# End of a decoder block: the last residual half rows added into the PSUM banks, outputs by one fused operation, third pass tile by tile

## The chip, the cores and the metric

The kernel runs on one core of a Trainium2 chip. The metric is device microseconds of one execution. The kernel before took a median of 804.33 us over three runs (804.27 to 804.5). The core has five engines that work beside each other: TensorE (PE in the profile; PEld are its weight loads) multiplies into PSUM banks, VectorE (DVE) and ScalarE (ACT) do element work and can read and write PSUM, GpSimd (POOL) helps early in the kernel, and SyncE (SP) issues nearly all DMAs.

## The reference, cut to what matters

One decoder block on 512 tokens of width 1024: token mixers, then a SwiGLU feed-forward layer, then a final norm. The change concerns the last product and the final norm alone:

```python
def rmsnorm(x, g):
    y = x * rsqrt(mean(x * x, axis=-1, keepdims=True) + EPS)
    return y * g
...
x = x + m @ w_mix_out                                   # residual stream, 512 x 1024
h = rmsnorm(x, norm2_g)
x = x + (silu(h @ ffn_w1) * (h @ ffn_w3)) @ ffn_w2      # ffn_w2 is 2816 x 1024
return rmsnorm(x, norm_f_g)
```

All of it is float32.

## The kernel before, in words

**Products.** Each float32 operand is split into a high part (rounded to a format that TensorE multiplies fast) and a low part (the rest): `split_to` makes the high part by a copy on ACT (L122) and the low part by a subtraction (L118), for the weights of the end on DVE. A product of two tiles is then three matmuls: high times high, high times low, low times high.

**The last product** (`Sevenfold` with `outq`) is a two by two block product done with seven block products instead of eight. The 512 tokens are four tiles of 128; tiles 0 and 1 are the upper block row and tiles 2 and 3 the lower one. The 1024 output columns are two halves, h = 0 and 1, of 512 columns, the size of one PSUM bank. The inner dimension has 11 steps (k = 0 to 10). The weights are quarters of ffn_w2 (`b11`, `b21`, `b22`, ...) and sums of quarters (`t1` to `t4`) that the kernel made much earlier and stored in DRAM. Weights come through a ring of four raw buffers and a ring of five split buffers, one chunk after the other in a fixed order (`wchunk`, `get`, `weights`).

`run` makes three passes over k. The first fills banks `r1`, `r2` and `r5` (two banks each, i = 0 and 1). The second (`second`) goes on in `r1` with `t2`, and fills a new `r2` and `r7`. The third (`third`) goes on in `r1` with `t4`. What stands in `r1[i]` after each pass is part of a different output: after the third it is the product for token tile 2 + i, column half 0.

`x2[t][h]` (the profile's `x2b`) holds the residual stream of token tile t and column half h, reloaded from DRAM. `plus(t, h, bank)` adds a bank to it on DVE (`add`, L883).

**The end** (`out_end`, L1202 to L1225) runs after the first pass: `second`; then the sums that tiles 0 and 1 still lack; then `finish(0)` and `finish(1)`; then `r7` is added to tiles 2 and 3; then the third pass with k from 0 to 7, each k for tile 2 and then tile 3; and at last, for tile 2 and then tile 3, `finish` with `rest`, which runs the third pass for k = 8, 9, 10 and adds `r1[i]` to column half 0.

**`finish(t)`** (L1178 to L1200) is the final norm of one token tile. `rstd_of` takes the sum of squares of the two halves on ACT (`Square` with `accum_out`, L534 and L540, each followed by a read of the accumulator), forms the mean plus epsilon (DVE L535), takes the root on ACT (L541) and the reciprocal on DVE (L542). Each half is multiplied by the gain `gf` on DVE (L1184) before the reciprocal is known, and by the reciprocal afterwards: one half on DVE (L1194), the other on ACT (L1198), for tile 2 both on DVE (L1196). Two DMAs of 256 KB store the tile (L1200, issued by SP).

**What sets the order.** The order of instructions on each engine is fixed when the program is built; a planner orders them by the order of writing and its own estimates. Each engine then takes its list strictly in order and waits where an operand is not there. SP's list of DMAs is in order too, and the output stores are the last in it.

Of the kernel before, what the change touches and what calls it, by code (L numbers as in the profile page):

```python
# [8 lines left out]
F32 = mybir.dt.float32  # L9
F32R = mybir.dt.float32r  # L10
AF = mybir.ActivationFunctionType
ALU = mybir.AluOpType
# [34 lines left out]
ADDING = ()  # L47
SUMS_FROM, SUMS_AHEAD = 5, 3
GATES_AT = 6
SUMS_AT, SUMS_STEP, SUMS_LAG, STORE_LAG = 4, 3, 2, 4  # L50


# [33 lines left out]
def tile_block(ctx, tc, a, out):  # L86
# [9 lines left out]
    def tiles(tag, bufs):  # L96
        p_ = pool(tag, bufs)
        return lambda name, dtype=F32: p_.tile([P, T], dtype, tag=tag, name=name)

    longt, shortt, gatet = tiles("long", SLOTS), tiles("short", SHORT), tiles("gate", GATES)  # L100

    def pairt(name, dtype=F32R):

        return longt(f"{name}h", dtype), longt(f"{name}l", dtype)

    def bank(name):
        return psum.tile([P, T], F32, tag="mm", name=name)
# [4 lines left out]
    vec, act, pe, pool_e = nc.vector, nc.scalar, nc.tensor, nc.gpsimd  # L112


    newest = {}

    def sub(eng, o, x, y):
        return eng.tensor_tensor(out=o, in0=x, in1=y, op=ALU.subtract)  # L118

    def split_to(h, l, full, eng, copy=act.copy):  # L120

        copy(h, full)  # L122
        last = sub(eng, l, full, h.bitcast(F32))
        if eng is pool_e:
            newest["sub"] = last.ins
        return h, l

    def split(name, full, eng, p_=None, copy=act.copy):
        p_ = p_ or pairt(name)
        return split_to(*p_, full, eng, copy)  # L130
# [9 lines left out]
    def emit_chunk():  # L140
        if emitted[0] == GATES_AT:
            load_gates()
        key, src, kt, cols, where, lo, after = chunks[emitted[0]]
        emitted[0] += 1
        n = kt * cols
        if where == "made":
            raw = src()
        else:
            raw = raws.tile([P, 1024], F32, tag="raw", name=f"raw_{key}")
        rv = raw[:, :n]  # L150
        if where == "made":
            pass
        elif callable(src):
            src(raw)
        else:
            newest["load"] = nc.sync.dma_start(rv.rearrange("p (k n) -> p k n", k=kt), src).ins
        if where != "long":
            hl = hls.tile([P, 2, 1024], F32R, tag="hl", name=f"hl_{key}")
            h, l = split_to(hl[:, 0, :n], hl[:, 1, :n], rv, lo)
            if after:  # L160
                after(rv, h)
            held[key] = (h.rearrange("p (k n) -> p k n", k=kt), l.rearrange("p (k n) -> p k n", k=kt))
        else:
            held[key] = [
                split_to(longt(f"{key}h{i}", F32R), longt(f"{key}l{i}", F32R), rv[:, i * T : (i + 1) * T], lo)
                for i in range(2)
            ]
# [25 lines left out]
    def load_gates():  # L193
      with tc.issue_after(newest["load"]):
        for gi, name in enumerate(("lru_wa", "lru_wx")):
            nc.sync.dma_start(gate_rows[:, gi, :], a[name][0].rearrange("h r n -> (h r) n"))
# [205 lines left out]
    outq = Quartered("o", a["ffn_w2"][0].rearrange("(k p) n -> p k n", p=P), NF // 2, vec)  # L402
# [89 lines left out]
    first = [i for i, (lo, _, _) in enumerate(parts) if lo < n_first]  # L492
# [36 lines left out]
    def rstd_begin(half, junk):  # L529

        i = n_stats[0]
        n_stats[0] += 1
        ss, r = stats[:, i, :2], stats[:, i, 2:3]
        act.activation(junk, half, AF.Square, accum_out=ss[:, 0:1])  # L534
        vec.tensor_scalar(out=ss[:, 0:1], in0=ss[:, 0:1], scalar1=1.0 / D, scalar2=EPS, op0=ALU.mult, op1=ALU.add)  # L535
        return ss, r

    def rstd_end(begun, half, junk):
        ss, r = begun
        act.activation(junk, half, AF.Square, accum_out=ss[:, 1:2])  # L540
        act.activation(r, ss[:, 1:2], AF.Sqrt, scale=1.0 / D, bias=ss[:, 0:1])  # L541
        vec.reciprocal(r, r)  # L542
        return r

    def rstd_of(halves, junk, between=None):
        begun = rstd_begin(halves[0], junk[0])
        if between:
            between()
        return rstd_end(begun, halves[1], junk[1])
# [318 lines left out]
    for j in range(8):  # L868
        ws = w_tiles(f"lo{j}_0", 5) + w_tiles(f"lo{j}_1", 5)
        ps = bank(f"yb{j}")  # L870
# [12 lines left out]
    add = lambda o, x, y: vec.tensor_tensor(out=o, in0=x, in1=y, op=ALU.add)  # L883
# [100 lines left out]
    for n, j in enumerate(mixq.order()):  # L984
        ws = w_tiles(f"co{j}", ND)
        ps = bank(f"ya{j}")
        mm3(ps, ws, un)
        o = sga[j]
# [6 lines left out]
    x2 = [[longt(f"x2{t}{h}") for h in range(2)] for t in range(NT)]  # L995
# [66 lines left out]
    first = {}  # L1062
# [104 lines left out]
    x2 = [[longt(f"x2b{t}{h}") for h in range(2)] for t in range(NT)]  # L1167
    gf = pairt("gf", F32)
# [6 lines left out]
        for h in range(2):  # L1175
            nc.sync.dma_start(gf[h], a["norm_f_g"][h * T : (h + 1) * T].partition_broadcast(P))

    def finish(t, rest=None):  # L1178

        h = 1 if rest else 0  # L1180
        o = [shortt(f"of{t}{i}") for i in range(2)]

        def scaled(i):
            vec.tensor_tensor(out=o[i], in0=x2[t][i], in1=gf[i], op=ALU.mult)  # L1184

        def between():
            scaled(h)
            if rest:
                rest()
            scaled(1 - h)  # L1190

        r = rstd_of([x2[t][h], x2[t][1 - h]], [bank(f"jk{t}{i}") for i in range(2)], between)

        vec.tensor_scalar(out=o[1 - h], in0=o[1 - h], scalar1=r, scalar2=None, op0=ALU.mult)  # L1194
        if t == 2:
            vec.tensor_scalar(out=o[h], in0=o[h], scalar1=r, scalar2=None, op0=ALU.mult)  # L1196
        else:
            act.activation(o[h], o[h], AF.Copy, scale=r)  # L1198
        for i in (1 - h, h):
            nc.sync.dma_start(o_nat[:, t, i * T : (i + 1) * T], o[i])  # L1200

    def out_end(second, plus, r1, r2, r7, third):  # L1202
        kh, hold = outq.kh, 3
        second()
        for i in range(2):
            plus(i, 1, r1[i])
            plus(i, 1, r2[i])
            plus(2 + i, 1, r1[i])
        for i in range(2):
            finish(i)  # L1210
        for i in range(2):
            for h in (1, 0):
                plus(2 + i, h, r7[i])
        for k in range(kh - hold):
            for i in range(2):
                third(i, [k])
        for k in range(kh - hold, kh):
            outq.get(k, "t4")
        for i in range(2):

            def rest():
                third(i, range(kh - hold, kh))
                plus(2 + i, 0, r1[i])

            finish(2 + i, rest)  # L1225

    o7.run(x2, loads, out_end)


# [31 lines left out]
```

## Time and profile before

| what | value |
|---|---|
| median of three runs | 804.33 us (804.27 to 804.5) |
| the profiled execution | 805.56 us |
| its span in the trace | 803.8 us |
| PE busy | 790.0 us, 98% of the span |
| DVE busy | 678.6 us, 84% |
| ACT busy | 471.8 us, 59% |
| mean granted TensorE clock | 0.996 |

Times in the trace are microseconds from the start of the span. The profiled execution took 1.8 us more than its span (what lies around the traced instructions) and 1.2 us more than the median. PE is busy almost throughout, so the kernel's length is PE's work plus what stands before its first and after its last matmul. A row of a timeline reads: start, duration, engine, line, operation, output<-inputs, shape, and in brackets how long the engine sat idle before it and what ended the wait. Consecutive operations of DVE and of ACT overlap a little, so two rows can start closer together than one row is long.

### The profile page before, as it was taken

The page shows a single profiled execution, that of the slowest core. Times are in us where ns is not written, and L with a number is a line of the kernel's source. Part 1 is how long each engine was busy: PE and PEld are TensorE (multiplying, and loading weights), DVE is VectorE, ACT ScalarE, POOL GpSimd, SP SyncE. Part 2 cuts the span into 40 slices and gives each one's busy share as a digit, 9 for nine tenths or more (in the row PEclk, how much of TensorE's full clock was granted, in tenths as well). Part 3 has the DMA queues.
Part 4 walks back from the last instruction along what each step waited for, and adds up shares of the span by engine and source line. Part 5 has one row for each costly group of instructions (what it writes and reads, how often), then busy time and mean ns, then how long its engine had stood idle before and what let it go on. Part 6 is the DMA issues. An engine that isn't in the chain of part 4 may idle for free.

```text
span 803.8 us, 12199 instructions
## 1 busy us (share of the span) xinstructions
PE 790.0 (98%) x4374; PEld 690.7 (86%) x4374; DVE 678.6 (84%) x1034; ACT 471.8 (59%) x677; POOL 232.8 (29%) x182
## 2 busy tenths in 40 slices
PE   8999999999999999999999999999999999999996
PEld 7988888878888888888888888999999999888885
DVE  4699999999989988795887889977878887899756
ACT  7446595888668864573335574555455555577443
POOL 3565857686865855130000000000000000000000
PEclk9999999999999999999999999999999999999999
DMA  7845556477565764358947536467655553676652
GB/s 216 229 124 166 161 162 192 126 219 216 165 196 153 218 181 135 116 188 266 291 150 248 172 106 183 116 163 195 157 132 132 132 132 105 214 258 196 198 169 105
DMA packets 184624, 140.29 MB, mean 175 GB/s; under 512 B 14279, under 2 KB 162163, under 8 KB 184563
## 3 DMA queue, kind: packets, MB, share of 16 engines
q1 hardware_dynamic: 183123, 134.27, 55.7%
q0 software_dynamic: 1440, 5.24, 3.5%
q8 instruction: 34, 0.56, 0.3%
q14 instruction: 27, 0.22, 0.1%
HBM read 113.79 MB, written 18.64 MB: 165 GB/s over the span
## 4 chain that ended last, share of the span: by engine, by line
PE 82%; DVE 8%; DMA 4%; ACT 2%; SPq 1%; issue 1%; POOL 1%; ACTq 0%; POOLq 0%; DVEq 0%
PE z L518 28%; PE or L930 13%; PE ft L1057 7%; PE yb L518 7%; PE fa L1057 6%; PE ya L518 5%; PE mxr L930 5%; PE fe L1057 3%; PE fr L1057 3%; DVE cv L677 2%; PE fb L1057 2%; PE g L804 2%; DMA raw_in<-in_w_in_dram 2%; PE f L518 1%; DMA raw_fb<-in_ffn_w_dram 1%
## 5 line engine op out<-in xcount | busy, mean ns | idle before, releaser
L677 DVE SCALAR_TENSOR_TENSOR cv<-u,par,cv 128x511 f32<-128x511 f32 (+16 forms) x240 | 162.2, 730 | 2.7 <-ACT cv L674 2.5
L118 POOL TENSOR_TENSOR hl_in<-raw_in,hl_in 128x1024 fp32r<-128x1024 f32 x52 | 125.9, 2428 | 82.4 <-ACT hl_in L122 80.7
L344 POOL DMA_DIRECT2D raw_fb<-raw_fb x10 | 8.8, 875 | 300.0 <-DVE raw_fb L346 188.1
L118 POOL TENSOR_TENSOR ows<-ows 128x256 f32<-128x256 f32 x66 | 57.6, 875 | 37.1 <-DMA ows<-in_ffn_w_dram 34.1
L122 ACT CAST hl_in<-raw_in 128x1024 fp32r<-128x1024 f32 x52 | 54.2, 1043 | 11.5 <-PE z L518 6.6
L122 ACT CAST hl_ft<-raw_fb 128x1024 fp32r<-128x1024 f32 x40 | 41.9, 1049 | 31.2 <-DVE raw_fb L346 16.8
L118 DVE TENSOR_TENSOR hl_ft<-raw_fb,hl_ft 128x1024 fp32r<-128x1024 f32 x40 | 48.6, 1220 | 8.8 <-ACT hl_ft L122 8.7
L518 PE MATMUL z<-h10h,hl_in 128*128 128x512 f32 (+1 forms) x112 | 42.5, 381 | 1.5 <-ACT hl_in L122 1.2
L118 DVE TENSOR_TENSOR hl_fb<-raw_fb,hl_fb 128x1024 fp32r<-128x1024 f32 x30 | 36.6, 1221 | 8.7 <-ACT hl_fb L122 8.5
L518 PE MATMUL z<-h11h,hl_in 128*128 128x512 f32 (+1 forms) x112 | 41.9, 376 | 0.0
L518 PE MATMUL z<-h13h,hl_in 128*128 128x512 f32 (+1 forms) x112 | 41.9, 375 | 0.0
L518 PE MATMUL z<-h12h,hl_in 128*128 128x512 f32 (+1 forms) x112 | 41.9, 375 | 0.0
L518 PE MATMUL z<-h15h,hl_in 128*128 128x512 f32 (+1 forms) x112 | 41.8, 374 | 0.0
L518 PE MATMUL z<-h17h,hl_in 128*128 128x512 f32 (+1 forms) x112 | 41.7, 374 | 0.0
L518 PE MATMUL z<-h16h,hl_in 128*128 128x512 f32 (+1 forms) x112 | 41.7, 374 | 0.0
L518 PE MATMUL z<-h14h,hl_in 128*128 128x512 f32 (+1 forms) x112 | 41.7, 374 | 0.0
L346 DVE TENSOR_TENSOR raw_fb<-raw_fb,raw_fb 128x1024 f32<-128x1024 f32 x20 | 24.5, 1225 | 18.9 <-DMA raw_fb<-in_ffn_w_dram 18.7
L122 ACT CAST hl_fb<-raw_fb 128x1024 fp32r<-128x1024 f32 x30 | 31.4, 1046 | 6.9 <-PE mxr L930 3.7
L122 ACT CAST hl_ob<-raw_ob 128x1024 fp32r<-128x1024 f32 (+1 forms) x23 | 23.3, 1015 | 20.2 <-PE or L930 9.7
L118 DVE TENSOR_TENSOR hl_ob<-raw_ob,hl_ob 128x1024 fp32r<-128x1024 f32 (+1 forms) x23 | 27.0, 1174 | 9.5 <-ACT hl_ob L122 6.7
L1057 PE MATMUL fe<-hs_0h,hl_ft 128*128 128x256 f32 x160 | 30.8, 284 | 0.5 <-DVE hl_ft L118 0.5
L1057 PE MATMUL ft<-hs_1h,hl_ft 128*128 128x256 f32 x160 | 30.4, 284 | 0.0
(961 smaller groups left out, 2618.9 us busy)
## 6 DMA issues: line engine op xcount, KB each, us to landing
raw_in<-in_w_in_dram SPq DMA_DIRECT2D x52, 512.0 KB
raw_fb<-in_ffn_w_dram SPq DMA_DIRECT2D x96, 256.0 KB
ows<-in_ffn_w_dram SPq DMA_DIRECT2D x44, 256.0 KB
os<-ows SPq DMA_DIRECT2D x22, 512.0 KB
raw_ob<-in_ffn_w_dram SPq DMA_DIRECT2D x33, 256.0 KB
raw_ot<-os SPq DMA_DIRECT2D x33, 256.0 KB
raw_lo<-in_lru_w_out_dram SPq DMA_DIRECT2D x16, 320.0 KB
raw_fb<-raw_fb POOLq DMA_DIRECT2D x10, 512.0 KB, 4.5
```

The costliest lines, as they stand in the source:

```text
L118: return eng.tensor_tensor(out=o, in0=x, in1=y, op=ALU.subtract)
L122: copy(h, full)
L344: pool_e.dma_start(out=q, in_=y, accum_op=ALU.add)
L346: vec.tensor_tensor(out=q, in0=q, in1=y, op=ALU.add)
L518: pe.matmul(ps, l, r, start=i == 0, stop=i == n - 1)
L677: vec.scalar_tensor_tensor(out=acc[c][:, s:], in0=u[c][:, : T - s], scalar=dw(c, s), in1=acc[c][:, s:], op0=ALU.mult, op1=ALU.add)
L804: pe.matmul(ps, l, r, start=k == 0, stop=k == len(mms) - 1)
L930: pe.matmul(banks[i], l_[:, ts], r_, start=start and n == 0, stop=stop and n == 2, skip_group_check=again)
L1057: pe.matmul(ps[:, HALVES[i]], lw[:, 4 * i + c, :], rx_, start=not (again or i or c or m), stop=bool(i and c == 3 and m == 2), skip_group_c ...
```

## The change

Four things are edited; all of them lie in the end of the kernel.

1. **Third pass in blocks, tile by tile.** k = 0 to 3 for tile 2, then for tile 3; k = 4 to 7 for tile 2, then for tile 3. Before, the two tiles took turns at every k. The last block, k = 8 to 10, was and stays tile by tile.
2. **Residual into the bank.** `r7` is added to all four half rows of tiles 2 and 3 at once, half 0 first. After the block k = 0 to 3 of tile 2 + i, `x2[2 + i][0]` is added into the bank `r1[i]` on DVE; TensorE then goes on adding k = 4 to 10 to it. So at the end the bank holds the finished row half, and the addition after the last matmul is gone. The splits of later weights on DVE are held behind the first of these additions (`newest["tie"]`).
3. **Norm read from the bank, outputs fused.** `finish` for tiles 2 and 3 squares the half row out of the bank, and makes the output by one `scalar_tensor_tensor` (row times reciprocal times gain) instead of a `tensor_tensor` and a `tensor_scalar`. For tiles 2 and 3 the other half is still multiplied by the gain ahead of time and by the reciprocal on ACT; for tiles 0 and 1 both halves are fused operations on DVE.
4. **`finish(0)` and `finish(1)` moved** from before the third pass to after its block k = 4 to 7. The output tiles come from the large pool (`longt`) instead of the small one (`shortt`).

```diff
+SEED_AT = 4
...
     def split_to(h, l, full, eng, copy=act.copy):
         copy(h, full)
-        last = sub(eng, l, full, h.bitcast(F32))
+        if eng is vec and "tie" in newest:
+            with tc.issue_after(newest["tie"]):
+                last = sub(eng, l, full, h.bitcast(F32))
+        else:
+            last = sub(eng, l, full, h.bitcast(F32))
...
-    def finish(t, rest=None):
-        h = 1 if rest else 0
-        o = [shortt(f"of{t}{i}") for i in range(2)]
-        def scaled(i):
-            vec.tensor_tensor(out=o[i], in0=x2[t][i], in1=gf[i], op=ALU.mult)
-        def between():
-            scaled(h)
-            if rest:
-                rest()
-            scaled(1 - h)
-        r = rstd_of([x2[t][h], x2[t][1 - h]], [bank(f"jk{t}{i}") for i in range(2)], between)
-        vec.tensor_scalar(out=o[1 - h], in0=o[1 - h], scalar1=r, scalar2=None, op0=ALU.mult)
-        if t == 2:
-            vec.tensor_scalar(out=o[h], in0=o[h], scalar1=r, scalar2=None, op0=ALU.mult)
+    def finish(t, ps=None, rest=None):
+        o = [longt(f"of{t}{i}") for i in range(2)]
+        jk = [bank(f"jk{t}{i}") for i in range(2)]
+        first = x2[t][0] if ps is None else ps
+        begun = rstd_begin(x2[t][1], jk[0])
+        if rest:
+            vec.tensor_tensor(out=o[1], in0=x2[t][1], in1=gf[1], op=ALU.mult)
+            rest()
+        r = rstd_end(begun, first, jk[1])
+        vec.scalar_tensor_tensor(out=o[0], in0=first, scalar=r, in1=gf[0], op0=ALU.mult, op1=ALU.mult)
+        if rest:
+            act.activation(o[1], o[1], AF.Copy, scale=r)
         else:
-            act.activation(o[h], o[h], AF.Copy, scale=r)
-        for i in (1 - h, h):
+            vec.scalar_tensor_tensor(out=o[1], in0=x2[t][1], scalar=r, in1=gf[1], op0=ALU.mult, op1=ALU.mult)
+        for i in (0, 1):
             nc.sync.dma_start(o_nat[:, t, i * T : (i + 1) * T], o[i])
...
-        for i in range(2):
-            finish(i)
-        for i in range(2):
-            for h in (1, 0):
+        for h in (0, 1):
+            for i in range(2):
                 plus(2 + i, h, r7[i])
-        for k in range(kh - hold):
+        for k in range(SEED_AT):
+            outq.get(k, "t4", ahead=1)
+        for ks in (range(SEED_AT), range(SEED_AT, kh - hold)):
             for i in range(2):
-                third(i, [k])
+                third(i, ks)
+                if ks[0] == 0:
+                    seed = add(r1[i], r1[i], x2[2 + i][0])
+                    if i == 0:
+                        newest["tie"] = seed.ins
+        finish(0)
         for k in range(kh - hold, kh):
             outq.get(k, "t4")
+        finish(1)
         for i in range(2):
-            def rest():
-                third(i, range(kh - hold, kh))
-                plus(2 + i, 0, r1[i])
-            finish(2 + i, rest)
+            finish(2 + i, r1[i], lambda: third(i, range(kh - hold, kh)))
```

## The prediction

> **What bounds the kernel now.** I read the page first (shares of the engines, the chain that ended last), then the chain over the last 64 us in order of time, then the timelines of PE, DVE, ACT and SP from 780 us on, and at last the transfers in short windows behind the last matmul.
>
> ```profile
> PE 82%; DVE 8%; DMA 4%; ACT 2%; SPq 1%; issue 1%; POOL 1%; ACTq 0%; POOLq 0%; DVEq 0%
> ```
>
> ```profile
> 739.65 55.26 PE or L930 x241
> 794.91 0.02 issue
> 794.93 0.70 DVE x2b L883
> ...
> 796.97 0.28 DVE x2b L883
> ...
> 799.28 0.72 ACT of L1198
> ```
>
> The chain runs on PE without a break from 739.65 to 794.91. From there it goes over DVE and ACT to the last output tile. So only two things can move the time here: a new hole in PE before its last matmul, or the length of the tail behind it.
>
> ```profile
> 781.34 0.39 PE L930 MATMUL or<-hl_ot,oeb10l 128*128 128x512 f32 x1
> 781.72 0.70 PE L930 MATMUL or<-hl_ot,ovb0h 128*128 128x512 f32 x2
> ...
> 794.50 0.39 PE L930 MATMUL or<-hl_ot,ovb10l 128*128 128x512 f32 x1
> 794.73 0.62 PE L930 MATMUL or<-hl_ot,ovb8h 128*128 128x512 f32 x2
> ...
> 796.54 0.39 PE L930 MATMUL or<-hl_ot,ovb10l 128*128 128x512 f32 x1
> ```
>
> PE, one row each: the second pass ends, the third starts at 781.72, tile 2 ends with the matmul at 794.50, tile 3 with that at 796.54. From 794.50 to 796.54 are nine matmuls, 0.227 us each; a block of four k (12 matmuls) is 2.72 us, and the whole third pass (66) fills 781.72 to 796.77.
>
> The tail, first on DVE and ACT:
>
> ```profile
> 794.93 0.69 DVE L883 TENSOR_TENSOR x2b<-or,x2b 128x512 f32<-128x512 f32 x1 [2.86 <-PE or L930]
> ...
> 796.97 0.69 DVE L883 TENSOR_TENSOR x2b<-or,x2b 128x512 f32<-128x512 f32 x1
> ...
> 798.70 0.48 DVE L1196 TENSOR_SCALAR of<-of,stats 128x512 f32<-128x512 f32 x1
> 799.10 0.15 DVE L542 RECIPROCAL stats<-stats 128x1 f32<-128x1 f32 x1
> 799.29 0.49 DVE L1194 TENSOR_SCALAR of<-of,stats 128x512 f32<-128x512 f32 x1
> ```
>
> ```profile
> 796.29 0.58 ACT L534 ACTIVATE jk<-x2b 128x512 f32<-128x512 f32 x1
> 796.81 0.19 ACT L534 ACTIVATION_READ_ACCUMULATOR jk<-x2b 128x1 f32 x1
> 796.90 0.28 ACT L541 ACTIVATE stats<-stats 128x1 f32<-128x1 f32 x1
> 797.70 0.60 ACT L540 ACTIVATE jk<-x2b 128x512 f32<-128x512 f32 x1 [0.51 <-DVE x2b L883]
> 798.23 0.19 ACT L540 ACTIVATION_READ_ACCUMULATOR jk<-x2b 128x1 f32 x1
> 798.45 0.29 ACT L541 ACTIVATE stats<-stats 128x1 f32<-128x1 f32 x1
> 799.28 0.72 ACT L1198 ACTIVATE of<-of,stats 128x512 f32<-128x512 f32 x1 [0.54 <-DVE stats L542]
> ```
>
> After PE: add (796.97), square (797.70), root (798.45), reciprocal (799.10, late because DVE still scales tile 2 at 798.70), then both halves of tile 3 are scaled, on DVE until 799.78 and on ACT until 800.00. Then the stores (SP's rows, and windows whose last two columns are the busy share of the DMA engines and GB/s):
>
> ```profile
> 798.81 0.33 SPq L1200 DMA_DIRECT2D out_dram<-of  x1
> 799.24 0.90 SPq L1200 DMA_DIRECT2D out_dram<-of  x2
> 800.22 0.40 SPq L1200 DMA_DIRECT2D out_dram<-of  x1
> ```
>
> ```profile
> 799.00:799.60 0.60, 0.00 (x0) 0.00 (x0) 0.56 (x3) 0.32 (x1) 0.00 (x0) 1.00 0.00 0
> 799.60:800.00 0.40, 0.00 (x0) 0.00 (x0) 0.17 (x1) 0.40 (x1) 0.00 (x0) 1.00 0.91 333
> 800.80:801.20 0.40, 0.00 (x0) 0.00 (x0) 0.00 (x0) 0.00 (x0) 0.00 (x0) 0.78 1.04 379
> 802.00:802.40 0.40, 0.00 (x0) 0.00 (x0) 0.00 (x0) 0.00 (x0) 0.00 (x0) 0.50 0.96 364
> 802.40:802.80 0.40, 0.00 (x0) 0.00 (x0) 0.00 (x0) 0.00 (x0) 0.00 (x0) 0.50 0.07 21
> ```
>
> This is the part that the engines' shares hide: all four stores of tiles 2 and 3 are issued between 798.81 and 800.22, 0.42 us apart at the closest, and the data flow at some 380 GB/s without a gap from about 799.65 to 802.42. That is 2.77 us for four stores, 0.69 each: they queue, so the end goes by the first of the four, not by the last. Data start 0.84 us after an issue (798.81 to 799.65), and the span ends at 803.78, 1.36 after the last data.
>
> **The change, part by part.**
>
> *Third pass in blocks.* The same 66 matmuls in another order: 0 on PE, as long as each block finds its weights and its bank. Blocks on PE: tile 2 k0–3 781.72 to 784.44, tile 3 to 787.16, tile 2 k4–7 to 789.88, tile 3 to 792.60, then k8–10 as before. The split buffer that k = 10 reuses is free once tile 3 has done k = 1, now at about 785.8; its copy on ACT then ends near 786.6 and is wanted at 793.97. SP's list of loads has the same order and the same waits; no load moves.
>
> *Additions and seeds on DVE.* The page of time around them:
>
> ```profile
> 780.29 3.08 DVE L883 TENSOR_TENSOR x2b<-or,x2b 128x512 f32<-128x512 f32 x5
> 783.29 0.68 DVE L1184 TENSOR_TENSOR of<-x2b,gfl 128x512 f32<-128x512 f32 x1
> ...
> 788.46 2.95 DVE L118 TENSOR_TENSOR hl_ot<-raw_ot,hl_ot 128x1024 fp32r<-128x1024 f32 x3
> ```
>
> ```profile
> L883 DVE TENSOR_TENSOR fa<-fa,se 128x512 f32<-128x512 f32 x6 | 4.2, 692 | 0.0
> ```
>
> Five additions take 3.08 us, one every 0.60. The changed list has the four `r7` additions next: 783.29 to 785.69. The first seed follows. The trace has an addition into its own bank (`fa`, 692 ns), so the seed runs 785.69 to 786.38. PE saw a bank 0.15 us after DVE's last read of it (the second of the five additions, 780.89 to 781.57, then PE at 781.72), so PE may go on in that bank from 786.53 and wants it at 787.16: 0.63 us in hand. Behind the seed, in DVE's order, wait the splits of the later weights. k = 6 and 7 (1.2 us by the last row's three splits, two whole and one half): 786.3 to 787.5, its low part wanted at 788.75. The second seed can start when tile 3's block is through PE, near 787.4, and ends by 788.1, wanted at 789.88. The other two splits end near 789.9, wanted at 792.8 and 794.2. All of it is hidden behind PE; price 0, with 0.63 us as the thinnest cover. If that cover goes, each microsecond of delay is one on PE.
>
> *Norms of tiles 0 and 1, moved.* On DVE three small operations, two reciprocals, four fused operations and one gain product:
>
> ```profile
> L741 DVE SCALAR_TENSOR_TENSOR u<-z,par,sg x8: 741/748/750, 39.1 to 235.7; 128x512 f32<-128x512 f32 x8
> ```
>
> A fused operation of this size, out of a bank with a second operand, takes 748 ns, so the five large ones take some 3.5 us from 789.9, to about 793.8 with the small ones; DVE is next wanted at 796.2. The four squares on ACT fit into the time before 794.93, where ACT stood idle for 8.5 us before. Their four stores go out between about 791 and 794 and need 2.8 us of transfers, so they are through before tile 2's. Price 0; the cover is PE's last 3 us, and without it each fused operation would cost about 0.65.
>
> *The add after the last matmul, gone.* The built order on ACT at the end is: square of tile 2's bank, square of tile 3's other half, root of tile 2, scaling of tile 2's half 1, square of tile 3's bank, root, scaling. No row squares out of a bank; a copy of the same size out of a bank is a bound from below and the square from SBUF one from above:
>
> ```profile
> L1148 ACT COPY fb<-fa x6: 570/570/580, 571.1 to 671.3; 128x512 f32<-128x512 f32 x6
> ```
>
> 0.57 against 0.60 us; I take the square's own pace. Tile 2's bank is readable at 794.93 (where DVE started on it). Squares at 794.93 and 795.56 (796.29 less 795.66 is 0.63 a piece), root at 796.19. A root to a reciprocal that finds DVE free shows at the kernel's start:
>
> ```profile
> 5.65 0.29 ACT L541 ACTIVATE stats<-stats 128x1 f32<-128x1 f32 x1
> 5.97 0.16 DVE L542 RECIPROCAL stats<-stats 128x1 f32<-128x1 f32 x1 [1.47 <-ACT stats L541]
> ```
>
> 0.32 us. So reciprocal 796.51, and 0.18 later (799.10 to 799.28) ACT's scaling of tile 2 at 796.69 and DVE's fused operation beside it, both done near 797.43. ACT is free again 0.61 after, at 797.30. Tile 3's bank is readable at 796.97, so here the change adds a wait of 0.33 us: the square of tile 3 stands behind tile 2's scaling on ACT. Then square 797.30, root 798.06 (+0.76, as from 797.70 to 798.45), reciprocal 798.38 with DVE free, scaling on both engines at 798.57: ACT until 799.29, DVE (0.75 in place of 0.49) until 799.32. Before: 800.00. The add's 0.73 and DVE's delay of about 0.33 are saved, 0.33 is given back.
>
> *Stores.* Tile 2's are issued at 797.45 and 797.87 and flow from 798.29 to 799.68. Tile 3's are issued at 799.32 and 799.74, flow from 800.16 and, 2 x 0.69 later, end at 801.55. With 1.36 behind it the span ends at 802.91, 0.87 less than 803.78. The profiled execution, 805.56 with its span of 803.78, would become 804.69; it stands 1.23 above the median of 804.33, to which I apply the same difference: **803.46**.
>
> *A rule on stores.* The row shows stores that queue at 380 GB/s. The Trainium skill ("DMA: Bandwidth & Descriptors", the section on the anatomy of one DMA) gives each DMA, on GpSimd's path, a fixed cost of about 2.0 us, most of it the confirmation of the last byte, plus its bytes at 436 GB/s. By that rule the end would hang on the last issue rather than on the first, which is the second rival below; the trace's gapless 2.77 us speak for the queue.
>
> **Rivals.**
>
> *Seed too late, slower.* If the first seed is released only when tile 3's block is through as well (one wait for the whole group of PE work), it starts at 787.36, ends at 788.05, and PE goes on in the bank at 788.20 in place of 787.16: 1.04 us of hole, against 0.87 of gain, 804.50. In general PE is touched once the seed ends 0.63 late, and the kernel is slower than before from 1.50 late. For it speaks that PE already waits for DVE at this place (781.57 to 781.72) and that the cover is thin; against it, that the seed stands in DVE's list ahead of anything that needs tile 3's block. A further late seed would add to it; 0.05 for this, of which 0.04 over the bound.
>
> *The end follows the last issue.* If what ends the kernel is the last store's own latency, only its issue counts: 800.22 becomes 799.74, a gain of 0.48, **803.85**. The gapless transfer speaks against it. 0.13.
>
> *ACT not in the way.* If tile 3's square runs as soon as its bank is ready (796.97), everything after it is 0.33 earlier: 803.13. The built order speaks against it; some slack in each of the chained waits could give as much. 0.10.
>
> *More than the tail's gain.* From the last matmul's start to the span's end are 7.24 us, and without any wait on ACT the steps still need 6.04. To win over 1.6 us, something ahead of PE's end has to move too, of which there is only the hole of 0.15 at 781.57. 0.05.
>
> **How the numbers follow.** The forecast has the rest, 0.67, and its own range is 803.2 to 803.7. The range over the cases takes in the third and the second rival and half a microsecond of a late seed: 802.9 to 804.2. A measurement of this kernel can tell about 0.2% from no change, 1.6 us; the forecast and the middle rivals lie within that: same 0.91, faster 0.05, slower 0.04.
>
> **What would show it.** Right: no row of PE waiting on DVE between 781.8 and 796.8; last matmul still near 796.5; first seed done near 786.4; ACT's square of tile 3 starting 0.3 after its bank is ready; two separate bursts of transfers, the last ending near 801.55. Wrong: a hole in PE at 787.2 or 789.9, DVE still at tile 1's fused operations after 796.2, or a span that ends other than 1.36 after the last data.

## The result and the profile after

The changed kernel takes a median of 803.38 us (802.25 to 804.39, 21 runs) against 804.33 us (803.24 to 806.04, 21 runs) before: a ratio of 0.9986, with a 95% interval of 0.9980 to 0.9992. That is 0.95 us less; 0.87 was forecast. The interval leaves out 1, so the gain is real, and it lies within the 0.2% that the prediction took as the bound of no change.

The profiled execution took 803.2 us with a span of 801.42 us, 2.36 less than the 803.78 before. Not all of this is the change. The two timelines show where the difference arises. First PE after the change: end of the second pass, start of the third, tile 3's last matmul before PE returns to tile 2's bank and the return itself, last matmul of tile 2 and of tile 3.

```profile
779.91 0.39 PE L935 MATMUL or<-hl_ot,oeb10l 128*128 128x512 f32 x1
780.28 0.70 PE L935 MATMUL or<-hl_ot,ovb0h 128*128 128x512 f32 x2
...
785.59 0.39 PE L935 MATMUL or<-hl_ot,ovb3l 128*128 128x512 f32 x1
785.81 0.62 PE L935 MATMUL or<-hl_ot,ovb4h 128*128 128x512 f32 x2
...
793.07 0.39 PE L935 MATMUL or<-hl_ot,ovb10l 128*128 128x512 f32 x1
...
795.11 0.39 PE L935 MATMUL or<-hl_ot,ovb10l 128*128 128x512 f32 x1
```

The third pass starts 1.44 us earlier than before (780.28 against 781.72), and up to there the two kernels are the same. This part is chance: the profiled execution before took 1.23 us more than its kernel's median, the one after 0.18 less, and 0.96 of the 1.44 us stand there by the 308th of the 4374 matmuls, far ahead of the edits. Among the ten further profiles below, the third pass starts anywhere from 779.47 to 782.96. From its start to the last matmul are 14.83 us (before 14.82), and from the start of the last matmul to the end of the span 6.31 us (before 7.24). So the change is worth 0.93 us in the trace, all of it in the tail. Below, this **tail**, and the **third pass** from its first to its last matmul, are what the experiments are read by: they repeat to some hundredths, while the medians of ten runs move by some tenths for reasons that lie ahead of the change.

DVE after the change, in the third pass and the tail:

```profile
778.86 5.46 DVE L888 TENSOR_TENSOR x2b<-or,x2b 128x512 f32<-128x512 f32 x9
784.24 0.69 DVE L888 TENSOR_TENSOR or<-or,x2b 128x512 f32<-128x512 f32 x1
784.84 1.21 DVE L119 TENSOR_TENSOR hl_ot<-raw_ot,hl_ot 128x1024 fp32r<-128x1024 f32 x1
786.01 0.70 DVE L888 TENSOR_TENSOR or<-or,x2b 128x512 f32<-128x512 f32 x1
786.62 1.82 DVE L119 TENSOR_TENSOR hl_ot<-raw_ot,hl_ot 128x1024 fp32r<-128x1024 f32 x2
...
791.92 0.68 DVE L1190 TENSOR_TENSOR of<-x2b,gfl 128x512 f32<-128x512 f32 x1
...
796.89 0.16 DVE L547 RECIPROCAL stats<-stats 128x1 f32<-128x1 f32 x1 [0.33 <-ACT stats L546]
797.09 0.75 DVE L1193 SCALAR_TENSOR_TENSOR of<-or,stats,gfh 128x512 f32<-128x512 f32 x1
```

The rows `or<-or,x2b` are the two seeds. They take 0.69 and 0.70 us, the rows around them are the additions and splits between which the built order has them, and DVE has done everything for tiles 0 and 1 by 792.0, and tile 2's gain product by 792.6. Nothing is left between the last matmul and ACT's square. ACT in the tail:

```profile
793.49 0.58 ACT L545 ACTIVATE jk<-or 128x512 f32<-128x512 f32 x1 [4.47 <-PE or L935]
...
795.21 0.72 ACT L1195 ACTIVATE of<-of,stats 128x512 f32<-128x512 f32 x1 [0.23 <-DVE stats L547]
795.84 0.58 ACT L545 ACTIVATE jk<-or 128x512 f32<-128x512 f32 x1
796.35 0.18 ACT L545 ACTIVATION_READ_ACCUMULATOR jk<-or 128x1 f32 x1
796.56 0.29 ACT L546 ACTIVATE stats<-stats 128x1 f32<-128x1 f32 x1
797.09 0.72 ACT L1195 ACTIVATE of<-of,stats 128x512 f32<-128x512 f32 x1 [0.23 <-DVE stats L547]
```

Tile 2's bank is squared 0.42 us after its last matmul started (793.07 to 793.49). Tile 3's is squared 0.73 after (795.11 to 795.84): ACT scales tile 2 in between. Then the stores, in windows whose last columns are the busy share of the DMA engines and GB/s:

```profile
797.00:797.40 0.40, 0.00 (x0) 0.00 (x0) 0.36 (x2) 0.31 (x1) 0.00 (x0) 1.00 1.05 394
...
798.20:798.60 0.40, 0.00 (x0) 0.00 (x0) 0.00 (x0) 0.00 (x0) 0.00 (x0) 0.70 0.04 10
798.60:799.00 0.40, 0.00 (x0) 0.00 (x0) 0.00 (x0) 0.00 (x0) 0.00 (x0) 0.50 0.81 297
...
799.80:800.20 0.40, 0.00 (x0) 0.00 (x0) 0.00 (x0) 0.00 (x0) 0.00 (x0) 0.50 0.62 231
800.20:801.40 1.20, 0.00 (x0) 0.00 (x0) 0.00 (x0) 0.00 (x0) 0.00 (x0) 0.50 0.00 0
```

There are two bursts now, tile 2's and tile 3's, with a hole between them at 798.2 to 798.6, where before four stores ran on without one. The last data move at about 800.06, and the span ends 1.36 us later, as before. (Ends of data are read from the windows' shares, as if all DMA engines stopped together; the record of the last single packet ends some 0.1 us later in each kernel.)

So the 0.93 us divide into two parts. Tile 3's outputs are ready 2.73 us after the start of the last matmul (797.84 less 795.11) in place of 3.46 (800.00 less 796.54): 0.73. From there to the last data are 2.22 us in place of 2.42 (802.42 less 800.00), because tile 3's stores no longer queue behind tile 2's: 0.20.

### The profile page after: what moved, and what is told of

Its sections match the earlier page's. It is cut to its first block, busy times and chain, and to the rows that moved or that the text cites. A ratio compares the mean times of both kernels' runs of the same rounds, so it can differ in the third digit from the quotient of the medians.

```text
span 801.4 us, 12193 instructions
## 1 busy us (share of the span) xinstructions
PE 789.4 (99%) x4374; PEld 689.4 (86%) x4374; DVE 677.3 (85%) x1029; ACT 471.5 (59%) x676; POOL 232.3 (29%) x182
## 4 chain that ended last, share of the span: by engine, by line
PE 84%; DVE 8%; ACT 3%; DMA 2%; issue 1%; POOL 1%; SPq 0%; ACTq 0%; POOLq 0%; DVEq 0%
PE z L523 29%; PE or L935 13%; PE ft L1062 7%; PE yb L523 7%; PE fa L1062 6%; PE ya L523 5%; PE mxr L935 5%; PE fe L1062 3%; PE fr L1062 3%; DVE cv L682 2%; PE fb L1062 2%; PE g L809 2%; PE f L523 1%; DMA raw_fb<-in_ffn_w_dram 1%; DMA raw_in<-in_w_in_dram 1%
```

## The experiments

All are edits of the changed kernel; e8 to e10 contain e3's edit too. Third pass and tail are of one profiled execution each; the sum of the two is the kernel's last stretch. The ratios are to the kernel before, run on the same chip in the same series; e1 to e4, e5 to e8, and e9 with e10 are three series, so medians are not compared across them.

| kernel | third pass, us | tail, us | sum, us | median, us | ratio, 95% interval |
|---|---|---|---|---|---|
| before | 14.82 | 7.24 | 22.06 | 804.33 | 1 |
| changed | 14.83 | 6.31 | 21.14 | 803.38 | 0.9986, 0.9980 to 0.9992 |
| e1_no_seed | 14.85 | 7.23 | 22.08 | 803.59 | 0.9992, 0.9983 to 1.0001 |
| e2_seed_at_3 | 15.49 | 6.30 | 21.79 | 803.56 | 0.9994, 0.9985 to 1.0003 |
| e3_begin_early | 14.83 | 6.00 | 20.83 | 802.80 | 0.9981, 0.9972 to 0.9990 |
| e4_stores_together | 14.86 | 7.69 | 22.55 | 804.69 | 1.0003, 0.9994 to 1.0012 |
| e5_act_store | 14.82 | 6.43 | 21.25 | 803.75 | 0.9987, 0.9978 to 0.9997 |
| e6_norms_back | 17.10 | 6.32 | 23.42 | 808.15 (one run) | |
| e7_turns | 15.32 | 6.31 | 21.63 | 803.80 | 0.9995, 0.9986 to 1.0004 |
| e8_pieces | 14.85 | 6.35 | 21.20 | 803.72 | 0.9994, 0.9985 to 1.0003 |
| e9_whole_stores | 14.85 | 6.10 | 20.95 | 803.86 | 0.9989, 0.9980 to 0.9999 |
| e10_pieces_sp | 14.85 | 6.50 | 21.35 | 804.07 | 0.9995, 0.9985 to 1.0004 |

### Is it the seeds?

```diff
-                if ks[0] == 0:
-                    seed = add(r1[i], r1[i], x2[2 + i][0])
...
-            finish(2 + i, r1[i], lambda: third(i, range(kh - hold, kh)))
+            def rest():
+                third(i, range(kh - hold, kh))
+                plus(2 + i, 0, r1[i])
+            finish(2 + i, None, rest)
```

> The changed kernel without the seeds: the residual half row of tiles 2 and 3 is added on DVE after the last matmul again; blocks, moved norms and fused outputs stay. Measure: the tail, from the start of the last matmul to the end of the span (before 7.24 us, changed 6.31). If the gain comes from the seeds and the stores queue: DVE takes tile 3's add ahead of tile 2's reciprocal, all later steps move, outputs of tile 3 about 0.9 later and stores queue behind tile 2's: tail about 7.5, median about 1.2 above the changed kernel. If the end follows the last store's issue: tail about 7.25. If the fused outputs and moved norms carry the gain: tail stays near 6.3.

The tail is 7.23 us, that of the kernel before. DVE and SP of this kernel, whose last matmul started at 794.32:

```profile
794.75 0.69 DVE L888 TENSOR_TENSOR x2b<-or,x2b 128x512 f32<-128x512 f32 x1 [1.35 <-PE or L935]
795.36 0.15 DVE L547 RECIPROCAL stats<-stats 128x1 f32<-128x1 f32 x1
...
797.22 0.75 DVE L1193 SCALAR_TENSOR_TENSOR of<-x2b,stats,gfh 128x512 f32<-128x512 f32 x1
```

```profile
797.97 0.33 SPq L1199 DMA_DIRECT2D out_dram<-of  x1
```

The add stands behind the last matmul again, and ahead of tile 2's reciprocal. Tile 3's outputs are ready at 797.97, 3.65 after the last matmul's start, 0.92 later than in the changed kernel. So without the seeds nothing is left of the gain; blocks, moved norms and fused outputs together are worth nothing by themselves. This nothing is a balance: tile 3's outputs are ready 0.19 us later than in the kernel before (3.65 against 3.46), and its stores, which do not queue here, are through 0.19 us sooner after them. The median agrees less well: the ratios of e1 and of the changed kernel differ by 0.0006, about 0.5 us where 1.2 was expected, and their intervals overlap. The 7.5 that the queue was to give here did not come: this kernel's list has tile 2's stores out early enough (their data end at 798.6, tile 3's begin at 798.81), so nothing queues, and the run does not tell the two views of the stores apart. e4 does.

### How thin is the seeds' cover?

```diff
-SEED_AT = 4
+SEED_AT = 3
```

> The changed kernel with blocks k = 0 to 2 and 3 to 7 (SEED_AT = 3): PE wants the first bank back 1.36 us earlier. By the prediction's cover of 0.63 us the seed is then late by 0.73: one hole of about 0.73 us on PE ahead of tile 2's k = 3, tail unchanged at 6.3, median about 0.7 above the changed kernel. If the cover were larger than worked out (over 1.36): no hole; if the seed came late already in the changed kernel's sense (released with tile 3's block): a hole of about 0.9 or more.

PE of this kernel, and the two seeds on DVE:

```profile
785.46 0.39 PE L935 MATMUL or<-hl_ot,ovb2l 128*128 128x512 f32 x1
786.20 0.73 PE L935 MATMUL or<-hl_ot,ovb3h 128*128 128x512 f32 x2 [0.35 <-DVE or L888]
```

```profile
785.46 1.28 DVE L888 TENSOR_TENSOR or<-or,x2b 128x512 f32<-128x512 f32 x2
```

PE waits for DVE ahead of tile 2's k = 3, at the place and by about the amount expected: the third pass is 0.66 us longer (15.49 against 14.83), 0.73 was expected. From start to start the hole is 0.51 us (785.46 and 0.23 for one matmul, to 786.20), and the next matmul comes 0.11 late; the 0.35 in the row counts from the modelled end of the matmul before. With the bank wanted 1.36 earlier, the cover in the changed kernel is 1.36 - 0.66 = 0.70 us. Read from the changed kernel's own rows it is 0.73: the seed ends at 784.93, PE could go on 0.15 later, and does at 785.81.

### Had the norms of tiles 0 and 1 to move?

```diff
+        finish(0)
+        finish(1)
         for h in (0, 1):
             for i in range(2):
                 plus(2 + i, h, r7[i])
...
-        finish(0)
...
-        finish(1)
```

> The changed kernel with the norms of tiles 0 and 1 back ahead of the third pass, where they stood before. On DVE their fused operations (four, about 0.67 each) and reciprocals then stand ahead of the seeds. By the order of DVE's list the first seed ends about 3.0 us later than in the changed kernel, against a cover of 0.63: a hole of about 2.3 us on PE ahead of tile 2's k = 4, tail unchanged. If the move was only tidying: no hole.

```profile
788.26 0.39 PE L935 MATMUL or<-hl_ot,ovb3l 128*128 128x512 f32 x1
790.64 0.70 PE L935 MATMUL or<-hl_ot,ovb4h 128*128 128x512 f32 x2 [1.99 <-DVE or L888]
```

```profile
789.14 0.75 DVE L1197 SCALAR_TENSOR_TENSOR of<-x2b,stats,gfl 128x512 f32<-128x512 f32 x1
789.80 1.29 DVE L888 TENSOR_TENSOR or<-or,x2b 128x512 f32<-128x512 f32 x2
```

With the fused operations ahead of them the seeds start 6.84 us after the third pass did (789.80 less 782.96; 3.96 in the changed kernel), and the third pass is 2.27 us longer; 2.3 was expected. In e1, without the seeds, the move brought nothing, and without the move the seeds would cost more than they bring. The one time of this kernel, 808.15, is longer still because its third pass started 2.68 us later than in the changed kernel's profile; 2.45 of that stand there by the 308th matmul, long before anything that is edited.

### Are the blocks needed?

```diff
-            for i in range(2):
-                third(i, ks)
+            for k in ks:
+                for i in range(2):
+                    third(i, [k])
+            for i in range(2):
                 if ks[0] == 0:
                     seed = add(r1[i], r1[i], x2[2 + i][0])
```

> The changed kernel with the two tiles taking turns at every k again through k = 7; the seeds stay behind k = 3 of both tiles. In the built list of DVE three small operations that wait for ACT now stand ahead of the first seed, so it ends about 0.6 later than in the changed kernel, and PE wants the bank at the same time: hole 0 to 0.2 us, tail 6.3. If the blocks themselves are needed: a hole of about the time of one seed and its wait, 0.7 us or more.

```profile
784.91 0.70 DVE L888 TENSOR_TENSOR or<-or,x2b 128x512 f32<-128x512 f32 x1 [0.59 <-PE or L935]
```

```profile
784.48 0.39 PE L935 MATMUL or<-hl_ot,ovb3l 128*128 128x512 f32 x1
...
785.16 0.39 PE L935 MATMUL or<-hl_ot,ovb3l 128*128 128x512 f32 x1
785.76 0.70 PE L935 MATMUL or<-hl_ot,ovb4h 128*128 128x512 f32 x2 [0.20 <-DVE or L888]
```

The third pass is 0.49 us longer, more than expected, and for another reason than DVE's list: here DVE waits for PE (0.59 us) before the seed. When the tiles take turns, PE leaves a bank alone for three matmuls only, 0.68 us, and the seed with the waits on both sides of it does not fit in there: from the start of tile 2's last matmul (784.48) to the seed are 0.43 us, the seed takes 0.70, and PE goes on 0.15 later. That is 1.28 us, where four matmuls would have taken 0.91. In blocks PE is away for 2.72 us. So the blocks do earn their place, 0.49 us of it.

### Does ACT stand in the way?

```diff
+        for t in (2, 3):
+            early_rows[t] = begin_rows(t)      # o, jk and rstd_begin(x2[t][1], jk[0])
+            vec.tensor_tensor(out=early_rows[t][0][1], in0=x2[t][1], in1=gf[1], op=ALU.mult)
         for i in range(2):
             finish(2 + i, r1[i], lambda: third(i, range(kh - hold, kh)))
```

> The changed kernel with the square of tile 3's half 1, and its gain product, done ahead of the last block instead of between tile 2's steps. ACT then has 0.6 us less to do for tile 2 before tile 3's bank is ready. If tile 3's square stood behind ACT's work on tile 2 (0.30 us in the changed kernel's trace): square at once, about 0.43 after the last matmul's start, tail about 6.0, median 0.3 lower. If something else sets the end (the stores' queue, DVE): tail stays at 6.3.

```profile
795.38 0.39 PE L935 MATMUL or<-hl_ot,ovb10l 128*128 128x512 f32 x1
```

```profile
795.80 0.58 ACT L545 ACTIVATE jk<-or 128x512 f32<-128x512 f32 x1
```

Tile 3's bank is squared 0.42 us after its last matmul started, in place of 0.73, and the tail is 6.00, 0.31 less, as expected. The median is 802.80 us, a ratio of 0.9981 (0.9972 to 0.9990) to the kernel before: the lowest of all kernels here. Its gain over the changed kernel is read from the tail; the two were not run side by side.

### What ends the kernel: the queue of stores or the last store?

```diff
-        for i in (0, 1):
-            nc.sync.dma_start(o_nat[:, t, i * T : (i + 1) * T], o[i])
+        def store():
+            for i in (1, 0):
+                newest["out"] = nc.sync.dma_start(o_nat[:, t, i * T : (i + 1) * T], o[i]).ins
...
+        if t == 2:
+            held_store.append(store)
+        else:
+            store()
+        if t == 3:
+            with tc.issue_after(newest["out"]):
+                held_store[0]()
```

> The changed kernel with tile 2's two stores held back behind tile 3's in SP's list, so that all four leave together; nothing is computed otherwise. If stores queue at some 380 GB/s: data from 0.84 after the first issue, 2.77 us without a gap, end 1.36 later: tail about 7.7 (1.4 more). If the end follows the last store's issue: four issues 0.42 apart instead of two, tail about 7.15 (0.84 more).

Windows behind the last matmul, which started at 794.73:

```profile
798.23:798.63 0.40, 0.00 (x0) 0.00 (x0) 0.00 (x0) 0.00 (x0) 0.00 (x0) 0.50 0.84 307
800.63:801.03 0.40, 0.00 (x0) 0.00 (x0) 0.00 (x0) 0.00 (x0) 0.00 (x0) 0.50 0.97 369
801.03:801.43 0.40, 0.00 (x0) 0.00 (x0) 0.00 (x0) 0.00 (x0) 0.00 (x0) 0.50 0.07 21
801.43:802.42 0.99, 0.00 (x0) 0.00 (x0) 0.00 (x0) 0.00 (x0) 0.00 (x0) 0.50 0.00 0
```

The tail is 7.69 us: 1.38 more, two stores of 0.69, and not the 0.84 of two issues. The data flow from about 798.3 to 801.05 without a hole. The other half of the question is whether an earlier last issue helps:

```diff
         for i in (0, 1):
-            nc.sync.dma_start(o_nat[:, t, i * T : (i + 1) * T], o[i])
+            q = nc.scalar if t == 3 and i == 1 else nc.sync
+            q.dma_start(o_nat[:, t, i * T : (i + 1) * T], o[i])
```

> The changed kernel with the very last store (tile 3, half 1) issued by ACT beside SP's, so that its issue no longer waits 0.42 us for SP. If the stores' data queue: the data still need 1.39 us from the first issue plus 0.84, tail unchanged at 6.3. If the end follows the last issue: tail about 5.9.

The issues of tile 3's two stores, behind a last matmul that started at 796.56:

```profile
799.29 0.40 ACTq L1200 DMA_DIRECT2D out_dram<-of  x1
799.32 0.33 SPq L1200 DMA_DIRECT2D out_dram<-of  x1
```

The tail is 6.43, not 5.9. Both stores are issued at once, and the tail is not shorter for it (0.12 longer). The stores of the end are a queue.

### A head start for the last stores

```diff
+        if t == 3:
+            for c in HALVES:
+                vec.scalar_tensor_tensor(out=o[0][:, c], in0=first[:, c], scalar=r, in1=gf[0][:, c], op0=ALU.mult, op1=ALU.mult)
+                nc.sync.dma_start(o_nat[:, t, c], o[0][:, c])
+            act.activation(o[1], o[1], AF.Copy, scale=r)
+            nc.scalar.dma_start(o_nat[:, t, T:], o[1])
+            return
```

> The kernel with the early squares (tail about 6.0 expected there), and in it tile 3's half 0 scaled and stored in two pieces of 256 columns, half 1's store issued by ACT. If the data queue from the first store on: the first piece is ready 0.33 us earlier, tail about 5.7. If what ends the kernel is the last operation or the last issue: tail near 5.9 to 6.0.

The tail is 6.35, 0.35 more than without the pieces (e3), where 0.3 less was expected. The data did start early, and the last packet ended 0.16 us earlier than in e3, counted from the last matmul's start, but the span ended 1.8 us after the last data. Two more kernels take the edit apart: e9 computes in pieces and stores half 0 whole, e10 stores in pieces and issues everything from SP.

```diff
                 # e9: one store behind the loop in place of two in it
+            nc.sync.dma_start(o_nat[:, t, :T], o[0])
...
                 # e10
-            nc.scalar.dma_start(o_nat[:, t, T:], o[1])
+            nc.sync.dma_start(o_nat[:, t, T:], o[1])
```

> The kernel with the pieces, but tile 3's half 0 stored as one store of 512 columns by SP; half 1's store still issued by ACT. It tells which of two edits cost the piece kernel its 0.35 us. If the stores of 256 columns (rows of 1 KB) end later behind their last data: here the span ends 1.36 after the last data again and the tail is about 6.0. If the store issued by ACT does it: 1.8 after the last data and a tail of about 6.4.

> The kernel with the pieces, all three stores of tile 3 issued by SP. If rows of 1 KB are what costs: the end again some 1.8 after the last data, tail 6.2 to 6.4. If the store issued by ACT was the cost: 1.36 after the last data, and with the first piece's head start a tail of about 5.85.

The last windows of e9, and those of e10:

```profile
799.72:799.92 0.20, 0.00 (x0) 0.00 (x0) 0.00 (x0) 0.00 (x0) 0.00 (x0) 1.00 0.66 236
799.92:801.22 1.30, 0.00 (x0) 0.00 (x0) 0.00 (x0) 0.00 (x0) 0.00 (x0) 0.59 0.00 0
```

```profile
800.02:800.22 0.20, 0.00 (x0) 0.00 (x0) 0.00 (x0) 0.00 (x0) 0.00 (x0) 0.50 0.43 154
800.22:801.92 1.70, 0.00 (x0) 0.00 (x0) 0.00 (x0) 0.00 (x0) 0.00 (x0) 0.50 0.00 0
```

In e9 the data end near 799.84 and the span 1.38 later; in e10 near 800.10 and 1.82 later. So it is not the store issued by ACT that makes the end late, and the two kernels that end late, e8 and e10, are those that store tile 3 in three pieces, two of them with rows of 1 KB in place of 2 KB. The numbers go the way of the first branch of both expectations (e10's tail, 6.50, lies a little above its 6.2 to 6.4), but the rows are not the cause. Behind its last store SP waits for all stores, one after the other (L1273). Here are SP's instructions of that list between the last data and the end of the list, in e10 (800.22 to 801.10) and in e9 (799.92 to 800.40):

```profile
L1273 SPq EVENT_SEMAPHORE  x8: 27/28/28, 800.6 to 801.0; - x8
```

```profile
L1273 SPq EVENT_SEMAPHORE  x2: 28/28/28, 800.0 to 800.3; - x2
```

By the trace's records each output store reports its landing on a semaphore, a counter that other instructions can wait for. The eight stores of the other kernels use eight of them (101 and 104 to 110), and SP waits for them in that order, so that the wait for the last store is the last. The ninth store of e8 and e10 uses 101 again. So SP's wait on 101, which stands ahead of seven others, now lasts until the last landing, and SP goes through the seven, though they are met by then, behind it, one each 0.06 us: 0.43 us. In e9 only the second of the two in the row waits for the last landing, and nothing stands behind it.

From the last landing to the end of the span are 0.89 us in e3 and e9, 1.32 in e8 and 1.33 in e10, while from the last packet to its landing are 0.35 us in e3, e9 and e10 and 0.43 in e8. And in e10 the store that lands last is half 1, whose rows are of 2 KB. The plainest comparison is e8 with e9, which differ by nothing but the split store: its last packet ends 0.26 us earlier, its landing takes 0.08 longer (why stays open), its list of waits 0.43 longer, and the tail is 0.25 longer. A split that leaves the wait for the last store at the end of the list was not run; taking the 0.43 off e8's tail gives 5.92 as an estimate, 0.08 less than e3.

## Why the prediction was right

The time came out at 803.38 where 803.46 was predicted, and the tail at 6.31 where its steps add up to 6.37 (802.91 less 796.54). That the medians meet within 0.08 us is in part luck, since the interval of the measured gain is 0.64 to 1.6 us; the steps in the trace are the stricter test. Point by point, in us from the start of the third pass or of the last matmul:

| step | predicted | measured |
|---|---|---|
| first seed ends, from the third pass's start | 4.66 | 4.65 |
| second seed ends | 6.4 | 6.43 |
| last split of weights ends | 8.2 | 8.16 |
| tiles 0 and 1 and tile 2's gain product done on DVE | 12.1 | 12.3 |
| tile 3's square, from the last matmul's start | 0.76 | 0.73 |
| tile 3's outputs ready | 2.78 | 2.73 |
| last data | 5.01 | 4.95 |
| end of the span | 6.37 | 6.31 |

**Third pass in blocks, seeds, moved norms: hidden.** No row of PE waits for DVE after the start of the third pass, which is as long as before. The cover that was worked out at 0.63 us measures 0.70 to 0.73 (e2). That the thin place is this one, and that each microsecond past it is one on PE, e2 and e6 show.

**The add gone, a wait behind ACT in its place.** e1 gives the whole gain to the seeds. The prediction's wait of 0.33 us of tile 3's square behind ACT's scaling of tile 2 measures 0.31, and e3 takes away just that.

**The stores.** That they queue, and that the hole between tile 2's and tile 3's is part of the gain, was read from the gapless transfer; e4 and e5 confirm it. The second rival, an end that follows the last issue, falls with them. So does, for this place, the rule of the Trainium skill ("DMA: Bandwidth & Descriptors", the anatomy of one DMA) read as a cost per store behind its issue: two more stores cost their data, 1.38 us, and not their issues, 0.84. That section of the Trainium skill, on GpSimd's path, also puts most of a fixed cost of about 2.0 us down to the confirmation of the last byte. The stores from SP here do not bear that out: in the changed kernel 0.84 us go by from tile 3's first issue to its first data, and 0.46 from the last data to the last landing that the trace records (800.52). The other 0.90 of the 1.36 us behind the last data are the program's own end.

**The other rivals.** The late seed did not occur in the changed kernel; e2 and e6 are what it would have looked like. The rival without ACT's wait is e3, a kernel of its own, and came out at the 6.04 us that the prediction had worked out for it, within 0.04.

What the prediction did not see is how little room the old order left. It priced the blocks as a reordering at 0 and did not ask what the seeds would cost without them; e7 shows 0.49 us.

## What to carry to other kernels

Behind the last matmul every operation on the chain to the last store counts in full, so add what is known early into the accumulating bank while the matmuls still run; the seed needs a stretch in which PE works on another bank, longer than the seed plus the waits on both sides (here 0.68 us was too little and 2.72 enough). Whatever else stands in that engine's list ahead of the seed must move behind it, or the gain turns into a hole on PE. At the very end look at the transfers too: spread the last stores so that they do not queue, keep what belongs to an earlier tile off the engine that the last tile needs next, and keep the wait for the store that lands last at the end of the list of waits that closes the program.

## What the runs showed of the hardware that was not expected

Where SP's list at the end of the program has the wait for the store that lands last is worth up to 0.43 us. Where it is the last wait, the span ended 0.89 to 0.90 us after the last landing (nine kernels); with one wait behind it, in e5, 0.96; with seven behind it, in e8 and e10, 1.32 and 1.33: 0.06 us for each wait that was already met. So cutting a last store in two, which let the last packet end 0.26 us earlier (e8 against e9), made the tail 0.25 us longer. A store issued by ACT beside one issued by SP brought nothing.
